# Placement of rotations, first queries, chunk squares, a gate addition and a low plane in an encoder block

## The chip, the cores and the metric

The kernel runs on one core of a Trainium2 chip. The metric is device time in microseconds (us) of one execution, over several runs. Five engines work side by side and each takes its own instructions in order: TensorE (PE, matmuls), VectorE (DVE), ScalarE (ACT), GpSimd (POOL) and SyncE (SP), which here issues nearly all transfers. An engine that waits for a result holds back everything that stands behind the waiting instruction in its own order.

## The reference

The reference is one encoder block on 1024 tokens of width 1024, in float32:

```python
h = layer_norm(x, ln0_g, ln0_b)
proj = h @ w_in[l] + b_in[l]                      # width 4352
qa, ka, va, qb, kb, vb, ga, gb = jnp.split(proj, IN_SPLITS, axis=-1)
qb = partial_rotary(qb...); kb = partial_rotary(kb...)   # first 16 of 64 dims
y_na = neighbourhood_attention(qa, ka, va, na_rpb[l]) @ w_branch_na[l]
y_swa = windowed_gqa_with_sink(qb, kb, vb, swa_sink[l]) @ w_branch_swa[l]
mixed = jax.nn.sigmoid(ga) * y_na + jax.nn.sigmoid(gb) * y_swa
h = layer_norm(ALPHA * h + mixed @ w_out[l] + b_out[l], ln1_g[l], ln1_b[l])
u = jnp.square(jax.nn.relu(h @ w_ff1[l] + b_ff1[l]))
h = layer_norm(ALPHA * h + u @ w_ff2[l] + b_ff2[l], ln2_g[l], ln2_b[l])
```

There are 8 heads of each attention, 64 wide; the windowed one (swa) has 2 key/value heads, so one chunk of 128 columns holds all its keys and another all its values, and each of its four chunks of queries holds two heads.

## The kernel before, in words

Matrices are multiplied as two float16 planes each, a high plane and a low plane (the rest after rounding), with three products: high by high, high by low, low by high. A group of 128 output columns of the input projection (a chunk, class `Chunk`, L222) needs eight 128-row blocks times three products, 24 matmuls, for each of two halves of 512 tokens, so 48 matmuls. They accumulate in PSUM banks of the tag `mm`, of which there are two. Before that its weights go through five steps (`Chunk.to`, L241): 1, ACT squares them and sums (L213); 2, PE adds the sums over partitions into a bank of the tag `t` (L193); 3, DVE (L199) and POOL (L200) make the scale; 4, ACT casts the high plane (L252); 5, DVE makes the low plane (L254). Three raw buffers take turns, so a chunk's load can only land when the chunk three places earlier has its low plane.

**The order around the change is written out by hand.** `fills` lists the chunks: keys of the windowed attention, its values, its first queries, its second queries, then gates, further queries, and the values and queries/keys of the neighbourhood attention. `plan` gives each chunk's load and steps a due time, counted in matmuls of the projections; `defer` puts them in a list, `pump(n)` issues n matmuls, and `flush` issues what is due. A first loop issues 188 matmuls (three chunks and 44 of the fourth) with a flush after every four. In it `residual0` also gives DVE eight multiplications and additions for the first two token groups, and SP eight stores. After it, 67 calls of `steps` mix attention with the projections: each issues the scores of one step (`part_a`: PE L754 and L755, DVE L756, banks `s` and `t`), 12 or 18 projection matmuls, exponentials and casts on ACT (`part_e`, L775 and L778), the low plane on DVE and transposes on SP (`part_l`, L787 and L790), and products with the values (`part_c`, PE L862). ACT also evacuates the projections there (L534, L595, L500, L478, L674), and makes high planes of queries and keys (L537 to L539), whose low planes DVE makes (L544, L545).

A rotation (`rope`) of half a chunk of windowed queries or keys is: evacuation by ACT (L595) into one of two buffers; `stream_shuffle` on DVE (L603); two multiplications and an addition, 128x512 in float32, on POOL (L605 to L607); then high planes on ACT and low planes on DVE (L636, L638, L656). In the first loop the whole rotation is issued at once, four matmuls after its evacuation; in `steps` it is spread, one operation a step.

The kernel starts with the layer norm of eight token groups: statistics on DVE (L139 to L141), the root on POOL (L147), scaling on ACT (L357), transposes on PE (L374), evacuation with a high plane (L383 on ACT or L386 on DVE) and a low plane (L387 on DVE or POOL). Interleaved, two gate chunks are projected; a loop over i from 0 to 20 orders this.

After attention come four pairs of gate chunks by a seven-product scheme, in which step i of pair p (`g_mm`, PE L1139, 12 matmuls) accumulates into a bank and `g_after` reads it (ACT L1201 or DVE L1204). Steps 7 and 4 of a pair use the same bank, so step 4 can't start before `g_after` of step 7. `g_sums`, `g_hi` and `g_lo` prepare weights (DVE L1108, ACT L1124, DVE L1128). Then come the branch projections, the output projection, and the two layers of the MLP (FF1, PE L1661; FF2, PE L2133) in the same scheme. In FF1, `tick` prepares the weights of the list `seq` in order: low plane of one entry (`lo1`, DVE L1588), high plane of the next (`hi1`, ACT L1585), sums of the one after (DVE L1626). `comb_hi` and `comb_lo` make the planes of a large activation operand (ACT L1886, DVE L1889); `after1` reads a finished bank (ACT L1761, DVE L1781).

Of the kernel before, what the change touches and what calls it, by code (L numbers as in the profile page):

```python
# [61 lines left out]
LO_ON = (2, 3, 4), (1, 3, 5)  # L62
RS = 3, 3.5, 4.5, 5.5
HI_AT = 1
PRE_AT = {8: (0, 1), 12: (0, 3), 16: (0, 4), 18: (0, 5), 20: (1, 1)}
KEPT = {3: 'whi0', 4: 'wlo0', 5: 'whi1', 6: 'wlo1', 7: 'raw', 8: 'raw'}
ON_DVE = 99
PREP = 5, 6, 7, 8, 8, 9, 10, 12, 13, 14, 15, 16
HI_ACT = (0, 2, 3, 4, 5), ()
ST0=2  # L70
NO_DVE = ()
NO0=4
N_GATES = (2,), (3,), (4,), (), (5, 6, 7)
# [19 lines left out]
def encoder_block(ctx, tc, x, w_in, w_br, w_out, w_ff1, w_ff2, par, rows, rpbp,  # L93
# [131 lines left out]
    class Chunk:  # L225
# [8 lines left out]
            chunks.append(self)  # L234

        def load(self, src, x=None):
            ks = slice(0, 8) if x is None else slice(2 * x, 2 * x + 2)
            nc.sync.dma_start(self.raw[:, ks], src[:, ks])
            return self
# [265 lines left out]
    def cols(c0):  # L505

        return w_in[B_V + (c0 - 1024) // P]
# [79 lines left out]
    def rope(ps, bias, back, half, then, late=D_ROPE):  # L587
        cs = slice(half * 512, (half + 1) * 512)
        b = []

        def evac():
            tag = ("x2", "wlo2")[n_rope[0] % 2]
            n_rope[0] += 1
            b.append((ap if tag == "x2" else wp).tile([P, 512], F32, tag=tag, name="qf", bufs=1))
            ACT.activation(b[0], ps, AF.Identity, bias=bias, scale=back)  # L595

        def turn():
            qf = b[0]
            qs = []

            def shuffle():
                qs.append(ap.tile([P, 512], F32, tag="vt", name="qs", bufs=1))
                DVE.stream_shuffle(qs[0], qf, SWAP)  # L603
            ops = [shuffle,
                   lambda: POOL.tensor_tensor(out=qf, in0=qf, in1=rt[:, 0, cs], op=ALU.mult),  # L605
                   lambda: POOL.tensor_tensor(out=qs[0], in0=qs[0], in1=rt[:, 1, cs], op=ALU.mult),
                   lambda: POOL.tensor_tensor(out=qf, in0=qf, in1=qs[0], op=ALU.add),  # L607
                   lambda: defer(4 if in_steps else late[1], lambda: hi(qf), late[2], lambda: lo(qf))]
            if in_steps:
                rope_ops.extend(ops)  # L610
                if len(rope_ops) == 5:
                    rope_ops.pop(0)()
            else:
                for op in ops:
                    op()
        hi, lo = then
        defer(0, evac, late[0], turn)
# [74 lines left out]
    def plan():  # L692

        def to(j, n):
            return lambda: got[j].to(n)
        ev = []
        for j in range(1, len(todo)):
            u = 48 * j
            t = (u - 96, u - 72, u - 44, u - 28) if j > 8 else \
                [200 + 40 * (j - 7) + x for x in (0, 24, 44, 64)] if j > 6 else \  # L700
                [20 * j - 24 + x for x in (0, 14, 30, 34)]
            if j > 8:
                ev.extend((u - 150 + 8 * x, 0, (j, x)) for x in range(4))
            elif j > 2:
                ev.append((max(20 * (j - 3) + 12, 2) + (30 if j > 6 else 0), 0, (j, None)))
            ev.extend((x, n, j) for x, n in zip(t, (1, 3, 4, 5)))
        for x, n, j in sorted(ev, key=lambda e: e[0]):
            if n == 0:
                defer(x, lambda j=j: fetch(*j))
            else:  # L710
                defer(x, to(j, n), pe=n == 3, only=n != 3)
# [169 lines left out]
    def fills():  # L881
# [8 lines left out]
            return cols(1536 + hp * P), lambda w: proj_swa_q(hp, w, swa_q)  # L890

        yield cols(2048), lambda w: proj_swa_k(w, swa_kv)
        yield cols(2176), lambda w: proj_swa_v(w, prm[:, C_VB:C_VB + 1], swa_v)
        yield swa_q_of(0)
        for i in range(3):
            yield swa_q_of(i + 1)
            for j in N_GATES[i]:
# [13 lines left out]
    with tc.manual_schedule(engines=MANUAL):  # L911
# [56 lines left out]
        for i in range(2 * NK + LAG + HB):  # L968
            if i < NK or NK + HB <= i < 2 * NK + HB:
                h, k = (0, i) if i < NK else (1, i - NK - HB)  # L970
                if i >= 6:
                    ln0_bank(h, k)
                for g in range(0 if i >= 6 else 3, 4):
                    ln0_t(h, k, g)
                ln0_turn(h, k)
# [14 lines left out]
            for j in range(4):  # L990
                if RS[j] == i:
                    ln0_rstd(4 + j)
            if ST0 <= i < ST0 + 4:
                ln0_stats(4 + i - ST0)
            for j in range(4):
                if RS[j] == i + .5:
                    ln0_rstd(4 + j)
            if NO0 <= i < NO0 + 4:
                ln0_norm(4 + i - NO0, i - NO0 in NO_DVE)
            for (h, w), lag in lags:  # L1000
                j = i - lag - h * NK
                if 0 <= j < NK:
                    if j == 0:
                        next(gates[h][w])
                    for _ in range(3):
                        next(gates[h][w], None)
# [301 lines left out]
        g_after(2, 7)  # L1308
        g_sums(1, 6)
        g_hi(1, 6)  # L1310
        g_lo(1, 6)
        g_sums(0, 6)
        g_hi(0, 6)
        g_do(3, 7)
        g_lo(0, 6)
        g_after(3, 7)

        def b_load(f):
            braw[f] = dma_w(w_br[f])
# [358 lines left out]
    with tc.manual_schedule(engines=MANUAL):  # L1678
# [164 lines left out]
        def lo1(p, i):  # L1843
            lo_t1(p, tws[p, i], source1(p, i))
# [18 lines left out]
        def tick():  # L1863
# [2 lines left out]
            n_prep[0] += 1  # L1866
            if 0 <= n < len(seq):
                p, i = seq[n]
                lo1(p, i)
                if i == 4 and N_HEAD + 2 <= p + 2 < NP:  # L1870
                    load1(p + 2)
                if i == 5 and N_HEAD + 2 <= p + 1 < NP:
# [26 lines left out]
        ff1_mm(2, 2)  # L1899
        comb_hi("S3")  # L1900
        tick()
        after1(2, 1)
        after1(2, 2)
        comb_lo("S3")
# [523 lines left out]
```

## Time and profile before

| | |
|---|---|
| median of 3 runs | 1255.53 us (1253.75 to 1255.96) |
| profiled execution, its own time | 1255.74 us |
| its span, first to last instruction | 1253.9 us |
| mean granted clock of TensorE | 0.993 |
| PE busy | 1222.4 us (97%) |
| DVE busy | 960.0 us (77%) |
| ACT busy | 841.8 us (67%) |
| POOL busy | 340.3 us (27%) |

The profile records one execution. In the timeline each row has start, duration, engine, line, operation, output and inputs, and the number of instructions merged; in square brackets stands how long the engine had been idle before, and what ended that. In the table by stretches, each row has the length, the busy time of each engine (with its number of instructions), the granted clock of TensorE, the DMA engines' busy share and GB/s. In the list of waits, each row has the waiting engine and line, what it waited for, total us, number of waits, and the longest.

### The profile page before, as it was taken

The numbers are of one execution on the slowest core, as the hardware profiler recorded it, in microseconds if no ns is written. First come the engines' busy times: TensorE is split into PE (matmuls) and PEld (weight loads), VectorE is DVE, ScalarE is ACT, GpSimd is POOL, SyncE is SP. The second block draws the span as 40 slices with busy tenths as digits, with TensorE's granted clock in tenths as the row PEclk, the third lists the DMA queues.
The fourth block names the chain that finished last, engine by engine and source line by source line (L and its number), as shares of the span: only waits on it lengthen the run. The fifth ranks groups of instructions, "written<-read, shape, count | busy, mean of one in ns | idle before, by whom it ended". The sixth has DMA issues, their size and how long they took to land.

```text
span 1253.9 us, 16974 instructions
## 1 busy us (share of the span) xinstructions
PE 1222.4 (97%) x6024; PEld 671.9 (54%) x6024; DVE 960.0 (77%) x1373; ACT 841.8 (67%) x1353; POOL 340.3 (27%) x351
## 2 busy tenths in 40 slices
PE   8989999999999989999999999999999999999997
PEld 5535665555555437888884444444444444444443
DVE  6667997788886965444788977778857778898888
ACT  7557899898886555442567877787776746344457
POOL 4353231342430002335631013432300001211207
PEclk9998999999999999999999999999999999999999
DMA  8563678768665225647233457766627635363333
GB/s 323 160 210 74 149 158 190 161 149 174 158 149 177 92 90 202 202 134 263 107 151 110 134 194 246 247 231 235 215 108 263 218 135 227 126 260 126 126 110 135
DMA packets 177877, 216.83 MB, mean 173 GB/s; under 512 B 111744, under 2 KB 125312, under 8 KB 171136
## 3 DMA queue, kind: packets, MB, share of 16 engines
q1 hardware_dynamic: 176816, 214.89, 54.6%
q8 instruction: 47, 0.77, 0.3%
q10 hardware_dynamic: 976, 0.87, 0.2%
q14 instruction: 38, 0.31, 0.1%
HBM read 130.69 MB, written 59.33 MB: 152 GB/s over the span
## 4 chain that ended last, share of the span: by engine, by line
PE 76%; DVE 11%; ACT 6%; issue 3%; POOL 2%; DMA 2%; POOLq 0%; ACTq 0%; DVEq 0%
PE ps_mm L418 15%; PE ps_o L1661 6%; PE ps_t L1661 6%; PE ps_mm L2133 5%; PE ps_mm L1661 5%; PE ps_s L2133 5%; PE ps_t L2133 5%; PE ps_o L2133 5%; PE ps_s L1661 2%; PE ps_o L862 2%; PE ps_t L408 1%; PE ps_o L408 1%; PE ps_t L410 1%; PE ps_t L409 1%; PE ps_o L410 1%
## 5 line engine op out<-in xcount | busy, mean ns | idle before, releaser
L418 PE MATMUL ps_mm<-hT 128*128 128x512 f16 x960 | 227.5, 381 | 5.4 <-POOL hT L387 2.1
L1661 PEld LDWEIGHTS <-tw 128*128 128x128 f16 x1248 | 122.1, 99 | 144.9 <-issue 1.5
L2133 PEld LDWEIGHTS <-hS 128*128 128x128 f16 x1008 | 98.7, 98 | 118.2
L418 PEld LDWEIGHTS <-hT 128*128 128x128 f16 x960 | 90.9, 100 | 103.7 <-issue 14.0
L775 ACT ACTIVATE ss<-ss,sk 128x384 f32<-128x384 f32 (+1 forms) x128 | 74.0, 579 | 27.8 <-DVE sk L756 27.2
L1661 PE MATMUL ps_t<-hS,tw 128*128 128x512 f16 x384 | 87.9, 379 | 0.0
L1416 POOL TENSOR_TENSOR mx<-sg 128x512 f32<-128x512 f32 x16 | 32.5, 2033 | 143.2 <-DVE sg L1415 143.2
L418 PE MATMUL ps_mm<-hT,wpair 128*128 128x512 f16 x288 | 71.2, 390 | 0.0
L1851 DVE TENSOR_TENSOR usl<-usl 128x512 f32<-128x512 f32 x64 | 52.4, 818 | 23.5 <-ACT usl L1779 23.3
L1582 POOL TENSOR_TENSOR c<-c 128x2 f32<-128x2 f32 x16 | 15.6, 976 | 193.3 <-DVE c L1581 193.3
L2153 POOL TENSOR_TENSOR acc<-acc,rst 128x512 f32<-128x512 f32 x16 | 29.0, 1811 | 126.1 <-DMA rst<-xr_d 118.2
L200 POOL TENSOR_TENSOR hT<-hT 128x2 f32<-128x2 f32 x30 | 25.2, 841 | 124.0 <-DVE hT L199 124.0
L1139 PEld LDWEIGHTS <-hT 128*128 128x128 f16 x336 | 33.3, 99 | 44.1 <-issue 6.3
L1966 DVE SCALAR_TENSOR_TENSOR hS<-stg,c,hS 128x2048 f16<-128x2048 f32 x21 | 50.0, 2379 | 7.9 <-ACT hS L1963 7.9
L1588 DVE SCALAR_TENSOR_TENSOR tw<-raw,c,tw 128x512 f16<-128x512 f32 x60 | 51.2, 853 | 4.2 <-ACT tw L1585 3.9
L2133 PEld LDWEIGHTS <-hA 128*128 128x128 f16 x336 | 32.8, 98 | 40.1 <-DVE hA L1966 0.7
L862 PE MATMUL ps_o<-pt,vv 128*128 128x256 f16 (+1 forms) x448 | 49.1, 250 | 0.1
L787 DVE SCALAR_TENSOR_TENSOR pl<-ss,pl 128x768 f16<-128x768 f32 (+1 forms) x42 | 46.5, 1107 | 1.3 <-ACT pl L778 1.1
L862 PEld LDWEIGHTS <-vv 128*128 128x128 f16 x448 | 35.4, 98 | 17.4 <-DVE oT L871 1.8
L1661 PE MATMUL ps_o<-hS,tw 128*128 128x512 f16 x192 | 44.0, 379 | 0.0
L1585 ACT ACTIVATE tw<-raw,c 128x512 f16<-128x512 f32 x60 | 41.8, 709 | 2.8 <-DVE raw L1626 2.8
L418 PEld LDWEIGHTS <-wpair 128*128 128x128 f16 x288 | 27.1, 101 | 29.8 <-issue 5.4
(398 smaller groups left out, 3111.4 us busy)
## 6 DMA issues: line engine op xcount, KB each, us to landing
us_d<-usl SPq DMA_DIRECT2D x112, 256.0 KB, 3.1
stg<-us_d SPq DMA_DIRECT2D x28, 1024.0 KB, 4.8
raw<-in_w_ff SPq DMA_DIRECT2D x24, 512.0 KB, 5.6
sg<-sg_d SPq DMA_DIRECT2D x32, 256.0 KB, 3.0
hA<-in_w_ff SPq DMA_DIRECT2D x8, 1024.0 KB, 7.5
hS<-in_w_ff SPq DMA_DIRECT2D x8, 1024.0 KB, 7.6
hT<-in_w_in SPq DMA_DIRECT2D x60, 128.0 KB, 2.5
hT<-in_w_in SPq DMA_DIRECT2D x11, 512.0 KB, 4.3
```

The costliest lines, as they stand in the source:

```text
L418: PE.matmul(ps, a[:, k, :], act(b, k), start=(k == 0 and i == 0), stop=(k == NK - 1 and i == 2))
L775: ACT.activation(p, p, AF.Exp, bias=nm[:, i:i + 1], scale=-1.0, accum_out=sums_l[o_chunk][:, hh, 2 * t + i:2 * t + i + 1])
L787: DVE.scalar_tensor_tensor(out=pl[:, n:2 * n], in0=e[:, 0:n], scalar=P_SCALE, in1=pl[:, 0:n], op0=ALU.mult, op1=ALU.subtract)
L862: PE.matmul(o, vs, move(part), start=(m == 0 and part == 0), stop=(m == len(runs) - 1 and part == 1))
L1139: PE.matmul(ps, w[:, a, k, :], act[:, b, k, :], start=(first and k == 0 and m == 0), stop=(k == 3 and m == 2), skip_group_check=True)
L1416: POOL.tensor_tensor(out=mx[:, f, half * 512:(half + 1) * 512], in0=both[0], in1=both[1], op=ALU.add)
L1585: ACT.activation(hi_lo(slot, 0), src, AF.Copy, bias=0.0, scale=w_scale(p))
L1588: DVE.scalar_tensor_tensor(out=hi_lo(slot, 1), in0=src, scalar=w_scale(p), in1=hi_lo(slot, 0), op0=ALU.mult, op1=ALU.subtract)
L1661: PE.matmul(ps, ww, act[:, part, k, :], start=(first and k == 0 and m == 0), stop=(k == 3 and m == 2), skip_group_check=True)
L1851: DVE.tensor_tensor(out=out, in0=a, in1=b, op=op)
L1966: DVE.scalar_tensor_tensor(out=slot[:, :, 1, :], in0=src, scalar=scale, in1=slot[:, :, 0, :], op0=ALU.mult, op1=ALU.subtract)
L2133: PE.matmul(ps, st[:, a, part, j * P:(j + 1) * P], w[:, a, wpart, :], start=(first and a == 0 and m == 0), stop=(a == 3 and m == 2), skip_ ...
```

## The change

- The three POOL operations of a rotation go to DVE where the rotation is issued in the first loop (both halves of the keys and of the first queries, the first half of the second queries). In `steps` they stay on POOL.
- The chunk of the first queries is projected before the chunk of the values.
- In `plan`, for chunks numbered 9 and up the square is due 16 matmuls earlier and the total and scale 12 earlier; casts are due as before; the four quarter loads are due at 152, 146, 140 and 134 matmuls ahead of the chunk instead of 150, 142, 134 and 126. For chunk 1, total, high and low plane are due 4, 6 and 6 matmuls earlier.
- In the first loop over i, the total and scale of chunk 0 are issued at the start of i = 12 instead of after its transposes and evacuation; the statistics of token group 7 are issued at the end of i = 4 instead of in i = 5.
- In the gates' scheme, step 7 of pair 3 and the addition that reads its bank are issued ahead of the low plane and sums that stood before them.
- In FF1, the low plane of the second entry of `seq` is issued before the two `after1` calls and the `comb_lo` that stood before it.
- An assertion on the use of the raw buffers is added; it issues nothing.

```diff
-PRE_AT = {8: (0, 1), 12: (0, 3), 16: (0, 4), 18: (0, 5), 20: (1, 1)}
+PRE_AT = {8: (0, 1), 16: (0, 4), 18: (0, 5), 20: (1, 1)}
...
-ST0=2
+STATS = {2: (4,), 3: (5,), 4: (6,)}
...
+            eng = POOL if in_steps else DVE
             ops = [shuffle,
-                   lambda: POOL.tensor_tensor(out=qf, in0=qf, in1=rt[:, 0, cs], op=ALU.mult),
-                   lambda: POOL.tensor_tensor(out=qs[0], in0=qs[0], in1=rt[:, 1, cs], op=ALU.mult),
-                   lambda: POOL.tensor_tensor(out=qf, in0=qf, in1=qs[0], op=ALU.add),
+                   lambda: eng.tensor_tensor(out=qf, in0=qf, in1=rt[:, 0, cs], op=ALU.mult),
+                   lambda: eng.tensor_tensor(out=qs[0], in0=qs[0], in1=rt[:, 1, cs], op=ALU.mult),
+                   lambda: eng.tensor_tensor(out=qf, in0=qf, in1=qs[0], op=ALU.add),
...
             u = 48 * j
-            t = (u - 96, u - 72, u - 44, u - 28) if j > 8 else \
+            t = (u - 112, u - 84, u - 44, u - 28) if j > 8 else \
                 [200 + 40 * (j - 7) + x for x in (0, 24, 44, 64)] if j > 6 else \
-                [20 * j - 24 + x for x in (0, 14, 30, 34)]
+                [20 * j - 24 + x for x in ((0, 14, 30, 34) if j > 1 else (0, 10, 24, 28))]
             if j > 8:
-                ev.extend((u - 150 + 8 * x, 0, (j, x)) for x in range(4))
+                ev.extend((u - 152 + 6 * x, 0, (j, x)) for x in range(4))
...
         yield cols(2048), lambda w: proj_swa_k(w, swa_kv)
+        yield swa_q_of(0)
         yield cols(2176), lambda w: proj_swa_v(w, prm[:, C_VB:C_VB + 1], swa_v)
-        yield swa_q_of(0)
...
+                if i == 12:
+                    got[0].to(3)
                 for g in range(0 if i >= 6 else 3, 4):
                     ln0_t(h, k, g)
                 ln0_turn(h, k)
...
-            if ST0 <= i < ST0 + 4:
-                ln0_stats(4 + i - ST0)
+            for j in STATS.get(i, ()):
+                ln0_stats(j)
...
             if NO0 <= i < NO0 + 4:
                 ln0_norm(4 + i - NO0, i - NO0 in NO_DVE)
+            if i == 4:
+                ln0_stats(7)
...
         g_hi(1, 6)
+        g_do(3, 7)
+        g_after(3, 7)
         g_lo(1, 6)
         g_sums(0, 6)
         g_hi(0, 6)
-        g_do(3, 7)
         g_lo(0, 6)
-        g_after(3, 7)
...
                 p, i = seq[n]
-                lo1(p, i)
+                if n != 1:
+                    lo1(p, i)
...
         comb_hi("S3")
         tick()
+        lo1(*seq[1])
         after1(2, 1)
         after1(2, 2)
         comb_lo("S3")
```

More of the change, by code (lines that the diff above doesn't have):

```diff
@@ L236, in load @@
         def load(self, src, x=None):
+            i = chunks.index(self)
+            assert i < 3 or chunks[i - 3].n == 5
             ks = slice(0, 8) if x is None else slice(2 * x, 2 * x + 2)
```

## The prediction

> **What bounds the kernel now.** I read the page first, then PE's waits, then the clock by stretches, then the timelines of all engines around each wait.
>
> ```profile
> span 1253.9 us, 16974 instructions
> PE 1222.4 (97%) x6024; PEld 671.9 (54%) x6024; DVE 960.0 (77%) x1373; ACT 841.8 (67%) x1353; POOL 340.3 (27%) x351
> ...
> PE ps_s L754 <- DVE q L656: 3.9, 1, 3.9
> PE ps_o L1139 <- DVE go L1204: 3.4, 1, 3.4
> PE ps_t L754 <- DVE sk L756: 3.0, 1, 3.0
> PE ps_t L193 <- ACT hT L213: 2.7, 2, 2.2
> PE ps_mm L418 <- POOL hT L387: 2.1, 3, 1.0
> PE ps_mm L1661 <- DVE twx L1588: 1.4, 1, 1.4
> PE ps_mm L418 <- DVE hT L386: 0.8, 1, 0.8
> PE ps_mm L418 <- DVE hT L254: 0.5, 2, 0.3
> PE ps_mm L1661 <- DVE usl L1781: 0.4, 1, 0.4
> ```
>
> PE is busy for all but 1253.9 - 1222.4 = 31.5 us. So the kernel's time is PE's work plus PE's gaps, and only what closes a gap counts. The listed gaps are single places, and each edit stands at one of them. A long gap costs more than itself: the granted clock (the column after POOL) falls behind it.
>
> ```profile
> 95.00:100.00 5.00, 3.90 (x11) 1.94 (x12) 3.70 (x7) 2.48 (x7) 4.51 (x3) 0.55 0.00 0
> 100.00:105.00 5.00, 5.00 (x20) 2.46 (x19) 2.04 (x7) 3.35 (x9) 0.21 (x1) 0.77 0.00 0
> ...
> 220.00:225.00 5.00, 2.68 (x7) 1.28 (x8) 4.94 (x11) 3.84 (x9) 1.39 (x2) 0.68 0.25 69
> ```
>
> After the gap at 92 to 96 us the lost clock is 3.90 x 0.45 + 5.00 x 0.23 = 2.9 us, after the one at 219 us 2.68 x 0.32 = 0.9 us. What a term below gains is the gap plus this.
>
> **The change part by part.**
>
> *Ahead of attention (rotations, order of chunks, chunk 1 earlier).* PE, then ACT, DVE, the group rows of POOL, and the whole stretch:
>
> ```profile
> 65.77 0.38 PE L193 MATMUL ps_t<-hT 128*128 128x2 f32 x2 [2.16 <-ACT hT L213]
> ...
> 82.59 9.66 PE L418 MATMUL ps_mm<-hT,wpair 128*128 128x512 f16 x44
> 96.10 0.58 PE L754 MATMUL ps_s<-kh,q 128*128 128x256 f32 x1 [3.86 <-DVE q L656]
> ...
> 103.13 2.76 PE L418 MATMUL ps_mm<-hT,wpair 128*128 128x512 f16 x12
> ...
> 60.32 1.15 ACT L252 ACTIVATE hT<-hT 128x1024 f16<-128x1024 f32 x1 [4.97 <-POOL hT L200]
> ...
> 74.24 1.06 ACT L213 ACTIVATE hT<-hT 128x1024 fp8e5<-128x1024 f32 x1 [1.95 <-DMA hT<-in_w_in]
> ...
> 49.96 2.73 DVE L337 TENSOR_TENSOR ln<-ln,r 128x512 f32<-128x512 f32 x4
> ...
> L605 POOL TENSOR_TENSOR qf<-qf,rt 128x512 f32<-128x512 f32 x6 | 9.3, 1545 | 4.9 <-DVE qs L603 4.9
> L606 POOL TENSOR_TENSOR qs<-qs,rt 128x512 f32<-128x512 f32 x5 | 8.9, 1770 | 0.0
> L607 POOL TENSOR_TENSOR qf<-qf,qs 128x512 f32<-128x512 f32 x5 | 7.5, 1505 | 0.4
> ...
> 47.00:92.00 45.00, 42.00 (x201) 19.39 (x199) 28.78 (x40) 24.71 (x38) 22.79 (x17) 1.00 0.54 181
> ```
>
> A rotation costs POOL 1.55 + 1.77 + 1.51 = 4.8 us. DVE does the same operation on the same shape in 2.73 / 4 = 0.68 us, so 2.05 us. Two things happen with it.
>
> First, the scale of chunk 2 (L200) stood behind the keys' rotation on POOL and held ACT for 4.97 us at 60.32; behind ACT stood the keys' evacuation, their four casts and the square of chunk 4, and PE waited for that square 2.16 us. On DVE the rotation ends 2.8 us sooner, but the two operations of `residual0` that ran beside it now come after it: 2 x 0.68 = 1.37 us. That chain gains some 1.4 us, and about 0.5 us more because L200, alone on POOL, need not wait: 1.9 us. PE also loses its wait for a low plane just before (about 0.3 us, L254), which chunk 1's earlier steps cover, so it arrives earlier, and the gap shrinks from 2.16 to 0.55 us. Gain 1.9 us. The next wait of this kind (the second of the 2.7 us, so 0.5 us) is ACT standing for a chunk's load at 74.24, which starts when a low plane frees its buffer; with DVE some 2.5 us ahead the load is early enough by about 0.4 us: gain 0.5 us.
>
> Second, the first scores at 96.10 waited for the first queries' second rotation, low plane last. They are now projected 48 matmuls earlier, 48 x 0.22 = 10.5 us (from 44 in 9.66). I follow DVE to their last low plane: rotations, low planes of keys and of chunks, in order, end at about 84 us, and PE reaches the scores at 89.5. So the 3.86 us and the 2.9 us of clock go: 6.8 us. In exchange the values are late: evacuated at about 82, maximum and high plane until 87, low plane until 88, transposes on SP until 91, landing some 3 us later. Their first use is three steps after the first scores; a step is 12 matmuls, 2.76 us, and scores, so at or after 99. Covered; without that cover, each us later costs a us of PE. On SP the values' transposes stood ahead of two chunk loads; they now follow them, and behind them come the first transposes of probabilities, some 4 us later.
>
> DVE takes on 5 rotations, 10.3 us, of which 8.2 fall into the stretch of the last row, where it was busy 28.8 of 45: 37 us of some 42. That is tight, and it bounds the term from below: if the removed waits return as waits for DVE, only the long gap goes, 6.8 us; all that is lost there is 0.3 + 2.16 + 0.5 + 6.8 = 9.8 us. I take 1.9 + 0.5 + 6.8 = **9.2 us**.
>
> *Squares, totals and loads of chunks 9 and up.*
>
> ```profile
> 217.85 0.28 PE L193 MATMUL ps_t<-hT 128*128 128x2 f32 x2
> ...
> 222.32 0.58 PE L754 MATMUL ps_t<-kh,q 128*128 128x256 f32 x1 [2.95 <-DVE sk L756]
> ...
> 214.53 1.05 ACT L213 ACTIVATE hT<-hT 128x1024 fp8e5<-128x1024 f32 x1
> ...
> 219.45 0.76 DVE L544 TENSOR_TENSOR kl<-hT,q 64x512 fp32r<-64x512 f32 x1 [3.04 <-ACT q L537]
> ```
>
> The gap has two causes. ACT had a square, a high plane, an evacuation and three casts in one step; DVE waited 3.04 us for the casts, with the scores' reduction L756 behind it. And the total at 217.85 had taken one of the two `t` banks, so the scores needed the other, not yet reduced. The square now comes two steps earlier, the total one, where the reduction before stands in front of the casts' low planes. Both causes go. I take the whole, 2.95 + 0.9 = **3.9 us**. From below: the work of ACT is only moved, so the lag can come back elsewhere, at a loss of as much as is gained in its clock, -1 us.
>
> By the Trainium skill, TensorE: Matmul & The Clock Gate, section HAM oscillation, it is PE-idle gaps over about 3.4 us that bring the clock down; by that this gap of 2.95 us would cost only itself, and the total gain were 0.9 us less. The trace disagrees: the clock is 0.68 in the 5 us around it.
>
> *Gate addition.*
>
> ```profile
> 434.64 7.93 PE L1139 MATMUL ps_o<-hT 128*128 128x512 f16 x36
> 446.00 4.25 PE L1139 MATMUL ps_o<-hT 128*128 128x512 f16 x12 [3.43 <-DVE go L1204]
> ...
> 440.06 0.69 DVE L1108 TENSOR_TENSOR gT<-graw 128x512 f32<-128x512 f32 x1
> ...
> 445.20 0.74 DVE L1204 SCALAR_TENSOR_TENSOR go<-ps_o,hT,go 128x512 f32<-128x512 f32 x1
> ```
>
> Step 4 of pair 3 waits for the addition that reads step 7. PE had finished step 7 after 24 of the 36 matmuls, at about 440; the addition stood behind two low planes and two sums until 445.20. It now follows the sum of 440.06, so it ends by 441.5, before PE has done the last 12. Gap gone, 3.43 us, and the slow clock behind it: 12 matmuls took 4.25 us there, 2.76 in the row of 103.13, so 1.5 us. The low planes move back by 0.74 us on DVE; the first is wanted 24 matmuls later. Taken **4.9 us**; bounds 3.4 and 5.2.
>
> *Low plane in FF1.*
>
> ```profile
> 684.61 2.33 PE L1661 MATMUL ps_mm<-hS,twx 128*128 128x512 f16 x10 [1.45 <-DVE twx L1588]
> ...
> 680.94 0.75 DVE L1781 SCALAR_TENSOR_TENSOR usl<-ps_s,c,sn 128x512 f32<-128x512 f32 x1 [2.33 <-ACT sn L1761]
> ...
> 683.80 0.75 DVE L1588 SCALAR_TENSOR_TENSOR twx<-ts,c,twx 128x512 f16<-128x512 f32 x1
> ```
>
> The low plane of 683.80 moves into the 2.33 us in which DVE stood idle. The gap of 1.45 us goes, but DVE has no idle time from there to 700 and is earlier by that one instruction, 0.67 us, not by 1.45; the wait of 0.4 us for L1781 (705 us) would take up the rest. I take **0.65 us**, bounds 0 and 1.45.
>
> *Start.* The waits for POOL L387 (longest 1.0) and DVE L386 (0.8) stand behind a scale on POOL and behind the statistics of group 7. Moved ahead, both fall; but the evacuations by ACT, without idle time there, give part back, and the low plane of block 5 comes about 0.5 us later. Between 0 and 1.8 I take the middle, **0.9 us**.
>
> Sum: 9.2 + 3.9 + 4.9 + 0.65 + 0.9 = 19.6 us. The profiled execution took 1255.74 us, 0.2 above the median, so the forecast is **1236 us**.
>
> **The rivals.**
>
> *Attention keeps a gap.*
>
> ```profile
> 150.00:175.00 25.00, 25.00 (x155) 15.37 (x154) 24.08 (x52) 23.50 (x50) 7.79 (x12) 1.00 0.66 149
> ```
>
> DVE (24.08 of 25) and ACT (23.50) are nearly full there; earlier PE gives them less time to catch up. A gap as at 219 stays or a like one opens: 3.9 us less, and one more of 2 us, so 1242. For it: their work is not less. Against: only one gap in 300 us so far.
>
> *DVE bounds the stretch ahead of attention.* 37 of 42 us in order, and the values last. Then that term falls to 6.8 and the values' first use waits some 5 us with its clock: about 9.2 - 2.4 - 7 = 0, so 1245. Against: `residual0` is over early and PE leaves DVE 5 us before the scores.
>
> *Slower: loads too late.*
>
> ```profile
> hT<-in_w_in SPq DMA_DIRECT2D x60, 128.0 KB, 2.5
> ```
>
> The last quarter of a chunk is now due 22 matmuls ahead of its square, not 30, at least 22 x 0.22 = 4.8 us, and it takes 2.5 us to land. If SP, in whose order transposes wait for DVE, is over 2.3 us late, the square stands, and exponentials behind it. There are 15 such chunks; from 19.6 / 15 = 1.3 us each on, all is lost. At 1.5 us the time is 1236 + 22.5 = 1259.
>
> *It doesn't do what it says:* the releasers are inferred, and the waits return with other names; 1255.
>
> **How the numbers follow.** Forecast 0.60, a gap in attention 0.22, DVE bound 0.11, loads 0.04, no effect 0.03. The forecast's own range is 1232 to 1240; the upper bounds of the terms, 9.8 + 3.9 + 5.2 + 1.45 + 1.8 = 22.2, give 1233.5, and 1231 leaves room for clock I don't count. To leave out no more than 2 in 10 it reaches over the second case to 1246. A measurement of this kernel tells 0.2% (2.5 us) from no change: faster 0.92, same 0.04, slower 0.04.
>
> **What would show it.** No wait of PE for L656 near 90 us, first scores near 88.5 us (with the start's gain), clock 1.00 there; no POOL rotation before them. The wait at L193 under 1 us. No PE gap over 1 us between 100 and 400. `ps_o` L1139 without a wait for L1204. L1661 without the 1.45, and a larger wait near 700 instead. It is wrong if PE's busy time grows, if the first product with the values (L862) waits, or if ACT waits for in_w_in in attention.

## The result, and the profile after

The changed kernel takes **1240.61 us** (median of 5 executions, 1239.58 to 1242.09), beside 1253.75 us for the kernel before (median of 5, 1253.19 to 1255.96). The ratio is 0.989, with a 95% interval of 0.9876 to 0.9905: 13.8 us faster (11.9 to 15.5). The forecast was 1236, so the time came out 4.6 us above it; of the 19.6 us of gain that it added up, 5.8 are missing. More is missing of the gain than of the time because the forecast started from an execution of 1255.74 us, 2.0 above before's median here. The profiled execution of after took 1239.58 us, 16.2 less than the profiled one of before.

The head of the page of after, and PE's waits there (waiting engine and line, what it waited for, total us, number, longest). Most lines stand 2 to 9 further down than before (L193 to L213 don't): L754 is now L757, L756 is L759, L862 is L865, L871 is L874, L544 is L546, L254 is L256, L1139 is L1146, L1661 is L1668, L1761 is L1768.

```profile
span 1237.8 us, 16985 instructions
...
PE 1215.5 (98%) x6024; PEld 669.7 (54%) x6024; DVE 963.7 (78%) x1388; ACT 840.7 (68%) x1353; POOL 319.6 (26%) x336
```

```profile
PE ps_mm L420 <- DVE hT L389: 2.0, 5, 1.0
PE ps_mm L420 <- POOL hT L389: 1.7, 4, 0.6
PE ps_o L865 <- DVE oT L874: 1.5, 1, 1.5
...
PE ps_t L1668 <- ACT sn L1768: 1.1, 1, 1.1
...
PE ps_mm L420 <- DVE hT L256: 0.7, 2, 0.5
PE ps_t L193 <- ACT hT L213: 0.7, 1, 0.7
PE ps_o L865 <- DVE oT L836: 0.6, 1, 0.6
PE ps_t L757 <- ACT rt L817: 0.6, 1, 0.6
PE ps_t L1668 <- DVE tw L1595: 0.4, 1, 0.4
PE ps_t L757 <- DVE sk L759: 0.3, 1, 0.3
```

The three longest waits of before (3.9, 3.4 and 3.0 us) are gone. New among these are 1.5 us for L874, 1.1 us for L1768, 0.6 us each for L836 (which scales a finished output of attention) and L817, and 0.4 us for the low plane L1595 in the bank `t`.

To see where the time came from I set the same PE instruction of both traces side by side; its start before minus its start after is PE's **lead**. The lead, part by part, worked out from those pairs of starts (39.85, 375.96, 450.47 and 435.09 are matmuls inside merged rows, counted on from the row's start):

| PE instruction, start before and after (us) | lead | gained since the row above |
|---|---|---|
| first half of the start, 39.85 and 39.34 | 0.5 | 0.5 |
| 12 matmuls after the second scores, 103.13 and 92.80 | 10.3 | 9.8 |
| products with the values after the gap at 219, 225.79 and 214.46 | 11.3 | 1.0 |
| last gap of after in attention, 375.96 and 365.84 | 10.1 | -1.2 |
| step after gate step 4 of pair 3, 450.47 and 435.09 | 15.4 | 5.3 |
| FF1, the matmuls that waited for L1781, 705.59 and 689.78 | 15.8 | 0.4 |
| end of the span, 1253.9 and 1237.8 | 16.1 | 0.3 |

These are differences of two single executions, and an execution can stray by 1 to 3 us in a part that no edit touches (see the account of the prediction); the medians of the experiments below say what a part is worth.

**Ahead of attention.** The timeline of after, one row each of ACT, DVE and SP's queue and then PE's rows (start, duration, engine, line, operation; in brackets the idle time before and what ended it):

```profile
57.89 1.15 ACT L254 ACTIVATE hT<-hT 128x1024 f16<-128x1024 f32 x1 [4.00 <-POOL hT L200]
...
81.91 1.40 DVE L659 TENSOR_TENSOR q<-qf,q 64x512 fp32r<-64x512 f32 x2
...
87.54 3.06 SPq L468 DMA_TRANSPOSE vv<-vv  x2
...
63.35 0.38 PE L193 MATMUL ps_t<-hT 128*128 128x2 f32 x2 [0.67 <-ACT hT L213]
...
88.72 0.47 PE L757 MATMUL ps_s<-kh,q 128*128 128x256 f32 x1
...
92.80 2.76 PE L420 MATMUL ps_mm<-hT,wpair 128*128 128x512 f16 x12
...
214.46 0.72 PE L865 MATMUL ps_o<-pt,vv 128*128 128x256 f16 x6 [1.53 <-DVE oT L874]
...
359.42 2.76 PE L420 MATMUL ps_mm<-hT 128*128 128x512 f16 x12 [0.53 <-DVE hT L256]
365.84 1.89 PE L420 MATMUL ps_mm<-hT 128*128 128x512 f16 x8 [0.34 <-ACT hT L677]
```

The scale L200 releases ACT at 57.89 where it was 60.32, the wait at L193 is 0.67 us where it was 2.16, and the first scores start at 88.72 without a wait where they started at 96.10 after 3.86 us. The same in the tables by stretches and by groups (POOL, 40 to 92 us): the clock stays at 1.00, DVE is busy 36.09 us of 48, and POOL has no rotation left, only the scales.

```profile
41.00:89.00 48.00, 47.33 (x227) 22.37 (x227) 36.09 (x60) 27.61 (x42) 4.53 (x6) 1.00 0.55 188
...
95.00:100.00 5.00, 5.00 (x27) 2.98 (x26) 3.77 (x7) 4.78 (x12) 1.41 (x2) 1.00 0.29 66
```

```profile
L200 POOL TENSOR_TENSOR hT<-hT 128x2 f32<-128x2 f32 x6 | 4.5, 755 | 35.6 <-DVE hT L199 35.6
```

**Attention.** The gap of 2.95 us is gone from its place, and the lead rises there by the gap and its clock, from 8.4 to 12.9. But PE meets the same late DVE 1.53 us later in the `o` bank (the row at 214.46), and by small waits it loses 1.9 us before that (10.3 down to 8.4), 0.6 of them at L836, and 1.2 us after it. DVE's timeline shows why:

```profile
208.74 0.69 DVE L546 TENSOR_TENSOR kl<-hT,q 64x512 fp32r<-64x512 f32 x1 [1.91 <-ACT q L539]
...
213.73 0.67 DVE L874 TENSOR_TENSOR oT<-ps_o,oT 64x512 f32<-64x512 f32 x1
```

It still stands for ACT's cast, 1.91 us instead of 3.04, with two reductions, a chunk's low plane and the addition L874 queued behind it.

**Gates and FF1.** PE's rows of after:

```profile
424.52 10.52 PE L1146 MATMUL ps_o<-hT 128*128 128x512 f16 x48
...
673.44 2.33 PE L1668 MATMUL ps_t<-hS,tw 128*128 128x512 f16 x10 [0.40 <-DVE tw L1595]
679.42 2.75 PE L1668 MATMUL ps_t<-hS,tw 128*128 128x512 f16 x12 [1.06 <-ACT sn L1768]
```

The 36 and 12 matmuls of the gates are one stretch of 48 in 10.52 us, which is 0.219 us each, full speed to the end. In FF1 the wait of 1.45 us is gone, and two waits of 0.40 and 1.06 us follow it a few us later.

### The profile page after: what moved, and what is told of

The parts are those of the page before. It is cut to its first block, busy times and chain, and to the rows that moved or that the text cites. A ratio compares the mean times of both kernels' runs of the same rounds, so it can differ in the third digit from the quotient of the medians.

```text
span 1237.8 us, 16985 instructions
## 1 busy us (share of the span) xinstructions
PE 1215.5 (98%) x6024; PEld 669.7 (54%) x6024; DVE 963.7 (78%) x1388; ACT 840.7 (68%) x1353; POOL 319.6 (26%) x336
## 4 chain that ended last, share of the span: by engine, by line
PE 78%; ACT 9%; DVE 7%; issue 2%; DMA 2%; POOL 1%; SPq 0%; ACTq 0%; POOLq 0%; DVEq 0%
PE ps_mm L420 14%; PE ps_t L1668 6%; PE ps_o L1668 6%; PE ps_s L2142 6%; PE ps_mm L2142 6%; PE ps_mm L1668 6%; PE ps_t L2142 5%; PE ps_o L2142 5%; PE ps_s L1668 3%; PE ps_o L865 2%; PE ps_o L1146 2%; ACT ss L778 1%; PE ps_mm L1146 1%; PE ps_t L1146 1%; PE ps_t L412 1%
## 5 line engine op out<-in xcount | busy, mean ns | idle before, releaser
L1668 PEld LDWEIGHTS <-tw 128*128 128x128 f16 x1248 | 122.0, 99 | 146.2 <-issue 2.1
L420 PEld LDWEIGHTS <-hT 128*128 128x128 f16 x960 | 90.6, 99 | 102.7 <-issue 12.7
L1668 PE MATMUL ps_t<-hS,tw 128*128 128x512 f16 x384 | 88.1, 379 | 1.5 <-ACT sn L1768 1.1
L420 PE MATMUL ps_mm<-hT,wpair 128*128 128x512 f16 x288 | 68.7, 380 | 0.0
L1589 POOL TENSOR_TENSOR c<-c 128x2 f32<-128x2 f32 x16 | 15.5, 976 | 193.3 <-DVE c L1588 193.3
L200 POOL TENSOR_TENSOR hT<-hT 128x2 f32<-128x2 f32 x30 | 26.4, 878 | 114.7 <-DVE hT L199 114.7
L1595 DVE SCALAR_TENSOR_TENSOR tw<-raw,c,tw 128x512 f16<-128x512 f32 x60 | 51.8, 864 | 5.1 <-ACT tw L1592 4.7
L1146 PEld LDWEIGHTS <-hT 128*128 128x128 f16 x336 | 32.9, 98 | 39.3 <-issue 0.4
L865 PE MATMUL ps_o<-pt,vv 128*128 128x256 f16 (+1 forms) x448 | 49.1, 250 | 2.3 <-DVE oT L874 1.5
L865 PEld LDWEIGHTS <-vv 128*128 128x128 f16 x448 | 35.5, 98 | 19.5 <-DVE oT L874 2.4
L1668 PE MATMUL ps_o<-hS,tw 128*128 128x512 f16 x192 | 44.0, 379 | 0.0
L2142 PE MATMUL ps_mm<-hA,hS 128*128 128x512 f16 x192 | 42.9, 379 | 0.0
```

The costliest lines, as they stand in the source:

```text
L420: PE.matmul(ps, a[:, k, :], act(b, k), start=(k == 0 and i == 0), stop=(k == NK - 1 and i == 2))
L865: PE.matmul(o, vs, move(part), start=(m == 0 and part == 0), stop=(m == len(runs) - 1 and part == 1))
L1146: PE.matmul(ps, w[:, a, k, :], act[:, b, k, :], start=(first and k == 0 and m == 0), stop=(k == 3 and m == 2), skip_group_check=True)
L1595: DVE.scalar_tensor_tensor(out=hi_lo(slot, 1), in0=src, scalar=w_scale(p), in1=hi_lo(slot, 0), op0=ALU.mult, op1=ALU.subtract)
L1668: PE.matmul(ps, ww, act[:, part, k, :], start=(first and k == 0 and m == 0), stop=(k == 3 and m == 2), skip_group_check=True)
L2142: PE.matmul(ps, st[:, a, part, j * P:(j + 1) * P], w[:, a, wpart, :], start=(first and a == 0 and m == 0), stop=(a == 3 and m == 2), skip_ ...
```

## The experiments

Of the five terms, only that for squares, totals and loads, 3.9 us, gave nothing in the trace. Two theories could be told apart. **First:** the new due times do close the gap near 219, and the lead of PE, or the other edits, bring small waits that eat the gain; then they are worth something where the other edits are missing. **Second:** they are worth nothing, because the gap comes from DVE standing for ACT's casts, and they only choose the bank at which PE meets it. The table has all twelve kernels; each ratio is against the kernel before on the same chip, whose median was 1253.76 (first four), 1255.85 (next four), 1256.33 (next three) and 1256.17 us (last).

| kernel | median us | ratio, 95% interval |
|---|---|---|
| `e1_old_plan` | 1239.62 | 0.9881, 0.9865 to 0.9897 |
| `e2_plan_alone` | 1255.34 | 1.0005, 0.9994 to 1.0015 |
| `e3_ahead_alone` | 1244.53 | 0.9926, 0.9909 to 0.9942 |
| `e4_gate_ff1_start` | 1248.63 | 0.9953, 0.9940 to 0.9966 |
| `e5_rotations_alone` | 1252.74 | 0.9978, 0.9966 to 0.9990 |
| `e6_order_alone` | 1249.91 | 0.9958, 0.9944 to 0.9972 |
| `e7_square_early` | 1239.64 | 0.9874, 0.9857 to 0.9892 |
| `e8_total_early` | 1241.06 | 0.9888, 0.9869 to 0.9907 |
| `e9_low_later` | 1239.37 | 0.9868, 0.9847 to 0.9889 |
| `e10_old_plan_low_later` | 1237.26 | 0.9854, 0.9837 to 0.9871 |
| `e11_old_plan_low_14` | 1237.56 | 0.9856, 0.9840 to 0.9872 |
| `e12_low_later_alone` | 1252.18 | 0.9973, 0.9962 to 0.9984 |

### The change without its due times

After, with the due times and loads of chunks 9 and up as they were:

```diff
-            t = (u - 112, u - 84, u - 44, u - 28) if j > 8 else \
+            t = (u - 96, u - 72, u - 44, u - 28) if j > 8 else \
...
-                ev.extend((u - 152 + 6 * x, 0, (j, x)) for x in range(4))
+                ev.extend((u - 150 + 8 * x, 0, (j, x)) for x in range(4))
```

> The changed kernel with the old due times of squares, totals and loads for chunks 9 and up; all else as changed. In the two traces PE's lead over the kernel before is 10.2 us when attention has begun, 8.5 us just ahead of the old gap at 219 us, 11.5 us behind it and 10.1 us when attention ends: the stage gave nothing, where 3.9 us was forecast. Theory A (the due times do what was forecast, and an earlier PE runs into DVE and ACT, which have no less work): with the old due times the gap of some 3 us in attention is back and the small ones stay; 1244 to 1246. Theory B (the new due times make the small gaps themselves, since the total now takes a bank of tag t in another step): the small gaps go, the gap of 3 us is back; 1239 to 1241.5, no different from the changed kernel.

It is as fast as the whole change (0.9881 beside 0.989). The gap is back at its old place, with DVE standing 3.03 us for the cast as before; DVE's and PE's rows, then the stretch of 5 us:

```profile
209.05 0.92 DVE L546 TENSOR_TENSOR kl<-hT,q 64x512 fp32r<-64x512 f32 x1 [3.03 <-ACT q L539]
...
212.09 0.39 PE L757 MATMUL ps_t<-kh,q 128*128 128x256 f32 x1 [2.10 <-DVE sk L759]
```

```profile
210.00:215.00 5.00, 2.50 (x13) 1.23 (x14) 4.96 (x10) 3.70 (x8) 2.14 (x5) 1.00 0.33 84
```

The price of the old due times is 2.10 us here, that of the new ones 1.53 us at L874 and small waits elsewhere for L817, L759 and L256, of which this kernel has 0.2 us in all. The clock stays at 1.00 behind this gap, so the 0.9 us for it aren't paid.

### The due times alone

Before, with the new due times and loads of chunks 9 and up (the diff above, turned round):

> The kernel before with the new due times for chunks 9 and up alone. Theory A: PE isn't earlier, so the gap at 219 us closes and no small one opens: 3 to 4 us faster, about 1250.5. Theory B: the small gaps open here too and eat the gain: 0 to 1 us faster, 1253 to 1254.5.

No difference that can be measured. The wait of 3.0 us for L756 is gone from PE's list, three others have come, and that for L254 has grown from 0.5 us:

```profile
PE ps_o L862 <- DVE oT L871: 1.4, 1, 1.4
...
PE ps_mm L418 <- DVE hT L254: 1.2, 3, 0.7
PE ps_t L754 <- ACT rt L814: 1.0, 1, 1.0
PE ps_t L754 <- DVE sk L756: 0.8, 3, 0.3
```

The waits for L871, L814 and L756 are after's waits for L874, L817 and L759, in a kernel without the edits ahead of attention; they come with the due times. So the first theory falls: alone, too, the due times are worth nothing. Two other small waits of after don't come with them. That for L836 stands in the kernel above as well (0.57 us at 171.84), and in none without the edits ahead of attention. The pair near 360 us, for the low plane L256 and for an evacuation, also stands in kernels with the old due times (`e4_gate_ff1_start` and `e10_old_plan_low_later`).

### The edits ahead of attention alone

Before, with the rotations, the order of chunks and chunk 1's due times:

```diff
+            eng = POOL if in_steps else DVE
...
-                [20 * j - 24 + x for x in (0, 14, 30, 34)]
+                [20 * j - 24 + x for x in ((0, 14, 30, 34) if j > 1 else (0, 10, 24, 28))]
...
+        yield swa_q_of(0)
         yield cols(2176), lambda w: proj_swa_v(w, prm[:, C_VB:C_VB + 1], swa_v)
-        yield swa_q_of(0)
```

> The kernel before with the rotations on DVE, the first queries ahead of the values, and the earlier steps of chunk 1; old due times else. The forecast's term is 9.2 us, and the trace of the changed kernel has 9.4 us there. Theory A: attention, entered 9 us earlier, gives up 1 to 2 us of it in small gaps, and the gap of 3 us stays: 1246 to 1247. Theory B: attention is as before: 1244 to 1245.

9.2 us between the medians (7.3 to 11.4 by the ratio's interval), where the term was 9.2. PE's list keeps the gap near 210; new in attention are 0.6 us for L834, after's L836, and 0.4 us right behind the gap for a scale's L199:

```profile
PE ps_t L755 <- DVE sk L757: 2.8, 1, 2.8
...
PE ps_o L863 <- DVE oT L834: 0.6, 1, 0.6
```

### Gate addition, FF1 and start alone

Before, with these three edits (as in the change's diff):

> The kernel before with the gate addition, the low plane in FF1 and the two moves at the start alone. By the forecast's terms 4.9 + 0.65 + 0.9 = 6.4 us; by the two traces 5.2 + 0.6 + 0.9 = 6.7 us: 1247 to 1248. A rival: the 0.9 us of the start is lost ahead of attention, where PE waits for the first queries' rotation whatever comes before: the chain to it starts with the keys' evacuation, which moves with PE, so 1247 again; if it is lost, 1248.5.

5.1 us between the medians and 5.9 by the ratio, where the three terms add up to 6.45. The wait for L1204 is gone; the new wait in FF1 is there with the same size as in after, and the wait at L193 is untouched:

```profile
PE ps_t L193 <- ACT hT L213: 2.2, 1, 2.2
...
PE ps_t L1665 <- ACT sn L1765: 1.1, 1, 1.1
```

The start is the only one of these edits ahead of the gates, and PE's lead at L193 is 0.45 us here (65.32 beside 65.77). In attention, which none of these edits touches, PE now waits 0.59 us for a chunk's low plane, and 0.35 us for an evacuation at 374.65:

```profile
368.24 2.76 PE L418 MATMUL ps_mm<-hT 128*128 128x512 f16 x12 [0.59 <-DVE hT L254]
```

Before has neither wait. Why they stand in this kernel and not in before stays open.

### Rotations alone, and order alone

The two large edits ahead of attention, one at a time, each on before:

```diff
+            eng = POOL if in_steps else DVE
...
-                   lambda: POOL.tensor_tensor(out=qf, in0=qf, in1=rt[:, 0, cs], op=ALU.mult),
+                   lambda: eng.tensor_tensor(out=qf, in0=qf, in1=rt[:, 0, cs], op=ALU.mult),
...
```

> The kernel before with the first loop's rotations on DVE alone; the values stay ahead of the first queries. If the rotation's engine is what counts: the wait for chunk 4's square falls from 2.16 to under 1 us, and the first queries' two rotations, 10 us one after the other on POOL, take some 5 us, so the wait at the first scores falls from 3.9 to 1 to 2 us with no slow clock behind it; 1246 to 1247. If it is the order that counts, the wait at the scores stays over 3 us with its slow clock; 1251 or more.

```diff
+        yield swa_q_of(0)
         yield cols(2176), lambda w: proj_swa_v(w, prm[:, C_VB:C_VB + 1], swa_v)
-        yield swa_q_of(0)
```

> The kernel before with the first queries ahead of the values alone; rotations on POOL. If the order is what counts: no wait at the first scores, no slow clock there, 6 to 7 us gone, but 2.16 us and 0.5 us of waits for squares stay: 1247 to 1248. If the rotation's engine counts: the first queries' buffer and DVE are still held by the keys' rotation on POOL, new waits for squares and low planes of 2 us and more open ahead of attention; 1250 or more.

The rotations alone give 2.8 us by the ratio, the order alone 5.3 us; 8.1 together, beside 9.2 for both with chunk 1. The order counts for more, though it gives less than the 6 to 7 us expected of it. The rotations on POOL were not the whole cause of the wait for the first scores: with none there it is still 3.6 us, beside 3.9 before. PE's list and ACT's timeline:

```profile
PE ps_s L755 <- DVE q L657: 3.6, 1, 3.6
```

```profile
91.71 0.78 ACT L595 ACTIVATE qf<-ps_mm,prm,hT 128x512 f32<-128x512 f32 x1 [4.13 <-DVE q L657]
92.39 1.24 ACT L652 CAST q<-qf 64x512 fp32r<-64x512 f32 x2
```

The evacuation of the second queries (91.71) needs one of two `qf` buffers and stands 4.13 us until the low plane of the first queries' first half has freed it. In ACT's order it is ahead of the casts of the first queries' second half (92.39), for which the scores wait. On DVE, too, the second queries' rotation (92.5 to 95.3) then stands ahead of the low planes that follow those casts (95.37). Projected earlier, the first queries have their casts done before that evacuation comes. In the kernel with the order alone the first scores start at 92.94 with no wait, and the 2.2 us at L193 stay. Rotations alone leave 1.22 and 1.45 us there at two chunks; with both, and chunk 1's due times, it is 0.7 us.

### One of the two due times, each alone

After with the square early and the total as of old, then after with the total early, the square at its old 96 and the old loads:

```diff
-            t = (u - 112, u - 84, u - 44, u - 28) if j > 8 else \
+            t = (u - 112, u - 72, u - 44, u - 28) if j > 8 else \
```

> The changed kernel with squares (and loads) of chunks 9 and up at the new due times and totals and scales at the old ones. If the total's new step makes the waits for banks of tag t (0.3 us at 142, 0.6 us at 191 us) these go; if the square's new step is what relieves ACT, the wait for L759 near 210 us, 2.1 us with the old due times, is under 1 us: then 1237.5 to 1239. If the two only work together, the wait near 210 is 2 us and the time as with all old due times, 1239.5.

```diff
-            t = (u - 112, u - 84, u - 44, u - 28) if j > 8 else \
+            t = (u - 96, u - 84, u - 44, u - 28) if j > 8 else \
...
-                ev.extend((u - 152 + 6 * x, 0, (j, x)) for x in range(4))
+                ev.extend((u - 150 + 8 * x, 0, (j, x)) for x in range(4))
```

> The changed kernel with totals and scales of chunks 9 and up at the new due times, squares and loads at the old ones. If the total's new step makes the waits for banks of tag t, they are all here (0.3 at 142, 0.6 at 191), and so are the late low planes near 360 us: 1240.5 to 1241.5. If it is the square's step that makes them, they are gone: 1239 to 1240.

Neither differs from after by more than the intervals (0.9874 and 0.9888). The places do. With the square alone early:

```profile
PE ps_t L757 <- DVE sk L759: 1.3, 1, 1.3
...
PE ps_o L865 <- DVE oT L874: 0.9, 1, 0.9
```

With the total alone early:

```profile
PE ps_t L193 <- ACT hT L213: 2.4, 3, 1.0
PE ps_o L865 <- DVE oT L874: 2.3, 1, 2.3
```

The total's step chooses the bank: at its old step the scores' bank `t` is taken and PE waits for L759; earlier, `t` is free and PE runs on into the `o` bank. The square's step sets how long DVE stands for the cast: 1.98 us with the square alone early, 2.97 with the total alone, beside 3.03 with both old and 1.91 with both early. What PE waits there for DVE stays much the same: 2.10 us with both old, 2.2 with the square early, 2.3 with the total early, 1.53 with both early. That last gain of some 0.6 us is paid for: the waits for L817, and the small ones for L759, come only with both early. With the total alone early they are waits at L193 for the square, 2.4 us in three where it was 0.7; that kernel's 1241.06 us lies where it was expected if the total makes the waits for `t`, but the waits behind that reading aren't there.

### The low planes later

If DVE's standing is the cause, it must help to let the low planes L546 and L547 be issued later, behind the reductions and the addition. `D_NA` is the number of matmuls between the casts of half a neighbourhood chunk and the issue of its low planes. After, then the kernel with the old due times, then the same with 14 instead of 8:

```diff
-D_NA = 4
+D_NA = 8
```

> The changed kernel with the low planes of the neighbourhood queries and keys (DVE L546, L547) due 8 matmuls behind their casts instead of 4, so that in steps of 12 matmuls they are issued behind the next step's reduction and low plane. Theory: what PE meets near 210 us is neither the bank of the total nor the bank of the products by itself, but DVE standing up to 3 us for ACT's casts with reductions and additions behind it; then the wait for L874 there (1.5 us) goes and the small ones at 142 to 191 stay: 1238.5 to 1239.5. Rival: DVE and ACT are simply full there, and the wait appears at another place: 1240 to 1241.5.

> The same with the old due times of squares, totals and loads (as in the run with the old plan, 1239.6). Theory: the wait for L759 near 210 (2.1 us) and the one behind it (0.4 us) go, and none of the small gaps of the new due times is there: 1236.5 to 1237.5, the fastest so far. Rival: 1239 to 1240.

> As the last, with 14 matmuls instead of 8, which also moves these low planes behind the reductions in the steps of 18 matmuls. PE has no gap there with the old due times, so by the theory nothing more is gained: 1236.5 to 1237.5. If DVE's standing costs there too without a gap that shows, 1236 or less; if low planes come too late for other work, 1238 or more.

With the old due times the gap near 210 goes altogether, and 1237.26 us (1236.57 to 1237.91) is the fastest time of all, below both kernels. DVE's timeline of `e10_old_plan_low_later`, and its stretches:

```profile
209.22 0.68 DVE L874 TENSOR_TENSOR oT<-ps_o,oT 64x512 f32<-64x512 f32 x1
209.92 0.69 DVE L546 TENSOR_TENSOR kl<-hT,q 64x512 fp32r<-64x512 f32 x1
```

```profile
205.00:210.00 5.00, 4.90 (x30) 3.11 (x29) 4.41 (x8) 4.87 (x10) 3.28 (x4) 1.00 0.99 242
210.00:215.00 5.00, 5.00 (x29) 2.80 (x28) 4.17 (x12) 4.90 (x12) 4.66 (x7) 1.00 1.00 184
```

L546 now comes behind L874 and stands for nothing, and PE is busy 5.00 us of 5 where it was busy 2.50. With the new due times the wait for L874 goes too, but waits of 1.6 us for L759 (three, the longest 1.1 at 359) and 0.7 us for L817 are there, and the kernel is 2.1 us slower than the one with the old due times. That one isn't free of small waits either: 0.84 us near 172 us for transposes, 0.70 and 0.34 us for the pair near 360. 14 matmuls give no more than 8.

### The low planes later, alone

The same edit on before, with nothing else:

> The kernel before with only the low planes of the neighbourhood queries and keys due 8 matmuls behind their casts instead of 4. If the gap at 219 us comes from DVE standing for the casts, it goes, and with it the slow clock: the forecast's 3.9 us, less 1 us if small waits remain, so a ratio of 0.997 to 0.998 to the kernel before. If the gap there needs an early PE, or the total's bank, to be read another way, it stays: ratio 0.9995 to 1.0005.

1252.18 us, ratio 0.9973: 3.4 us less (4.0 between the medians), which is about the 3.9 us that the forecast gave to the due times. The stretches around the old gap:

```profile
215.00:220.00 5.00, 5.00 (x34) 3.19 (x33) 4.76 (x10) 4.83 (x11) 4.78 (x9) 1.00 1.25 191
220.00:225.00 5.00, 5.00 (x32) 2.79 (x30) 3.83 (x10) 4.87 (x12) 1.50 (x2) 1.00 0.83 200
```

PE is busy throughout, at full clock, where before it was busy 2.68 us of 5 at 0.68. In this trace PE's lead grows by 4.6 us at the old gap (scores at 227.02 in before, 219.79 here, with a lead of 2.6 us ahead of it), and 1.6 us of it are lost in small waits by 390 us. That settles it for the second theory: DVE standing for the casts is the cause, and the place of the low planes, not that of squares and totals, is the edit that removes it.

## Why the prediction was right and wrong

**The frame was right.** PE's busy time plus its gaps is the kernel: of the 16.1 us of span, 31.5 - 22.3 = 9.2 are gaps (1237.8 - 1215.5 are left), and 1222.4 - 1215.5 = 6.9 are PE's busy time, with no matmul fewer, so matmuls that run faster where the clock was low.

**Ahead of attention, 9.2 us: right.** 9.8 us in the two profiled executions, of which 0.35 is the wait for the low plane that the term counted in; 9.2 us between the medians with these edits alone. Its parts came as told: scores at 88.72 (told: near 88.5), 0.67 us left at L193 (0.55), last low planes of the first queries at 83.3 (about 84), values' transposes until 90.6 (91), DVE busy 36.09 of 48 us. The rival that DVE bounds this stretch fell with that row. That the size agrees so well is partly luck. The term held 2.9 us of clock behind the scores, read from one execution. With no edit ahead of attention PE came to the second scores at 101.00 us in the kernel with the due times alone and at 99.28 us in that with the low planes later alone, where before's execution came at 102.12. Against that, these two lost 1.4 and 1.2 us of clock (4.23 x 0.34 and 4.22 x 0.28) behind the wait at L193, which the term put at nothing, as before's execution lost none there. What I hadn't seen is that the order does some 60% of it (5.3 of 9.2 us), and through ACT: the evacuation that stands for a `qf` buffer in front of the casts, and so also the rotation on DVE in front of the low planes. I had followed DVE alone.

**Squares, totals and loads, 3.9 us: wrong.** The failed step is "The square now comes two steps earlier, the total one, where the reduction before stands in front of the casts' low planes. Both causes go." The first cause, DVE waiting for the casts with work queued behind it, was named rightly, but it didn't go: 3.04 us became 1.91, since an exponential, a high plane and the casts are still ahead in ACT's order. The second cause, the taken `t` bank, did go, and what it brought is that PE met the same late DVE at the next bank. With the square early as well, the early total also put small waits for L759 and L817 into `t`. Measured alone the edit is worth 0 (1.0005); the 3.4 us are had by issuing the low planes later. My lower bound of -1 us for this term ("the lag can come back elsewhere") was within 1 us of it, and I took the upper end. The sign that failed with it is "No PE gap over 1 us between 100 and 400".

**The nearest rival** was "attention keeps a gap", 1242. 1240.61 lies 1.4 us from it, nearer than to the forecast, and 0.6 us above the forecast's own 1232 to 1240; the wider range held it because it reached over this case. Its reason, that earlier PE gives DVE and ACT less time to catch up, explains little: the 0.6 us at L836 stand only where the edits ahead of attention are in, but the due times alone show the waits for L871, L814 and L756 with PE where it was.

**Gate addition, 4.9 us: right**, 5.3 us in the trace, at its upper bound because the slow clock behind the old gap reached into the next step. Its 1.5 us of clock, too, were those of one execution (last section). **FF1, 0.65 us: right** in size, 0.7 us from 446 to the end of the span beyond the gates' part. The sign foretold, a larger wait near 700 for L1781, was wrong: that wait is gone, and PE waits for ACT's L1768 (1.06 us at 679) and the next low plane L1595 (0.40 us) instead. **Start, 0.9 us:** 0.5 us by the lead at 39.85, inside its bounds of 0 to 1.8, and 0.45 us in `e4_gate_ff1_start` ahead of the gates; it was not run by itself.

**Late loads** came twice in attention, 0.34 and 1.85 us, as the sign for it had said, but at no price; before has one of 0.75 us there. ACT's longer row of after:

```profile
314.69 1.06 ACT L213 ACTIVATE hT<-hT 128x1024 fp8e5<-128x1024 f32 x1 [1.85 <-DMA hT<-in_w_in]
```

PE doesn't wait for this square, and its lead is 11.3 us at 226 and still 11.3 us (369.37 and 358.06) just before the wait of 0.53 us at 359.42. That wait and the next, 0.34 us at 365.84, are for a chunk's low plane and an evacuation.

Of the 4.6 us between 1236 and 1240.61, 3.5 lie in the sum: -4.1 for this one term, -0.4 for the start, +0.6 ahead of attention, +0.4 for the gates. After's median is 1.0 us above its profiled execution; 0.1 is rounding.

## What to carry to other kernels

When PE waits for an engine that has been standing itself, look up the instruction at which that engine stood and what is queued behind it, and move that instruction; moving its neighbours in time changed, here, little but the bank at which PE met the delay. An instruction that needs another engine's fresh result belongs behind the work that needs nothing. And where a buffer has few copies, read each engine's whole order: here an evacuation that stood for a buffer was in front of the casts that everything waited for.

## What the runs showed of the hardware

The clock behind a gap isn't given by the gap. The same wait of 2.16 us, ending at the same 65.77 us, was followed by a clock of 1.00 in the profiled execution of before and of 0.66 in that of the due times alone. The stretch of before, then PE's row and the stretch of the due times alone:

```profile
65.00:70.00 5.00, 4.23 (x21) 2.10 (x22) 4.90 (x6) 4.96 (x9) 3.21 (x3) 1.00 1.00 393
```

```profile
65.77 0.54 PE L193 MATMUL ps_t<-hT 128*128 128x2 f32 x2 [2.16 <-ACT hT L213]
```

```profile
65.00:70.00 5.00, 4.23 (x13) 1.86 (x14) 4.90 (x6) 4.96 (x9) 3.20 (x3) 0.66 1.00 402
```

The price is 4.23 x 0.34 = 1.4 us in this stretch. It goes the other way too: the gap of 2.10 us with the old due times kept the clock at 1.00, and behind the first scores' wait (3.86 us before, 3.00 us with the low planes later alone) the clock was 0.55 and 1.00:

```profile
95.00:100.00 5.00, 3.82 (x20) 2.35 (x20) 3.79 (x7) 2.48 (x7) 4.43 (x3) 1.00 0.00 0
```

The gates' step 4 shows it best. Behind the same wait of 3.4 us its 12 matmuls took 4.25 us in before, 5.28 us with the low planes later alone, and 2.75 us, full speed, with the due times alone:

```profile
446.21 2.75 PE L1139 MATMUL ps_o<-hT 128*128 128x512 f16 x12 [3.42 <-DVE go L1204]
```

So the clock terms of the forecast, 2.9, 0.9 and 1.5 us, were read from one execution of before and are not paid in each. This fits that executions of before lie between 1251.73 and 1258.73 us over all runs, and those of the fastest kernel, whose longest gap behind the start is 1.1 us, between 1236.57 and 1237.91 (only four); that the clock alone makes this spread was not shown. The Trainium skill, TensorE: Matmul & The Clock Gate, Part 1, has the clock follow a free-running window of about 3.4 us, so that the same kernel varies from execution to execution. The runs agree with that; its rule in the section HAM oscillation, gaps over about 3.4 us, is too mild for them, with 0.66 behind 2.16 us; behind 3.42 us, at that bound, the clock stayed full once.
